# A decoder layer on one core: accumulating DMAs that read HBM, another choice of low parts made by DMA, and a single block split earlier

## The chip, the core and the metric

The kernel runs on one core of a Trainium2 chip. A core has TensorE (PE: matmuls, with weight loads, PEld, beside them), VectorE (DVE), ScalarE (ACT), GpSimd (POOL) and SyncE (SP), which only issues DMAs here; 16 DMA engines move data between HBM and the core's memory for all queues. Each engine works through its own instructions in the order in which they stand. The metric is the device time of one execution in microseconds, the median of several runs; lower is better.

## The reference

One layer of a decoder: heads of attention beside a convolution branch, an output projection, and a gated feed-forward part. All is float32; a batch of 1, 256 tokens, width 1024, feed-forward width 2816.

```python
def reference(x, norm1_g, w_in, glu_b, ..., w_out, norm2_g, w_gate, w_up, w_down):
    h = rms_norm(x, norm1_g[l])
    proj = h @ w_in[l]
    ...
    x = x + jnp.concatenate([attn, conv], axis=-1) @ w_out[l]
    h = rms_norm(x, norm2_g[l])
    x = x + (jax.nn.silu(h @ w_gate[l]) * (h @ w_up[l])) @ w_down[l]
    return x
```

The change touches the last line: `w_gate`, `w_up` and `w_down`.

## The kernel before

**Two parts of each number.** TensorE multiplies in a rounded float32 form. To keep float32 accuracy the kernel splits each operand into a high part (rounded) and a low part (what is left), and multiplies high by high, low by high and high by low. So each weight passes through three steps: a load from HBM into a raw place, the high part `wh` by ScalarE (L257), and the low part `wl`. The low part is made in one of two ways in `low_part`: VectorE subtracts (L219, raw less `wh`), or, for the pieces listed in `BY_DMA`, ScalarE writes the negated high part into `wl` (L216), and a DMA issued by GpSimd adds the raw weights to it (L217, `accum_op=add`). Before, that DMA reads the raw place.

**Pieces, blocks and places.** All weights lie in one HBM tensor `w` as 47 blocks of 128 x 2048, and a piece is 128 x 1024, so two pieces to a block. Blocks go into four raw places in turn (`RAW`), so block n + 4 overwrites block n: its load, on SyncE's queue (L196), waits until all that read block n are done, and the later loads stand behind it. High and low parts go into eight places (`WGT`); a new piece takes the one whose piece is oldest. Pieces 0 to 27 are for the projections, 28 to 71 for gate and up (a piece is one tile of 128 columns of one of them, in 22 steps `f`), and from `DOWN` = 72 on for the down projection.

**The down projection** goes in 11 pairs of 256 rows. The pairs marked F in `PAIRS` are done in seven products instead of eight (a scheme of Strassen's kind): three pieces and a *single block* of 512 columns. The first piece is the raw second half of the block; the other two are sums of blocks, the tile `t` that VectorE builds with three additions (`add_up`, L234 to L236). The single block is split by `single` (L200 on ScalarE for the high part, L201 on VectorE for the low), into `b11` for the even F pairs and into parts of the tile `other` for the rest. `single` also asks for the load of the block four further on. The P pairs have two plain pieces. Pair p uses block 36 + p:

| pair | kind | pieces | pair | kind | pieces |
|---|---|---|---|---|---|
| 0 | F | 72 to 74 | 6 | F | 88 to 90 |
| 1 | F | 75 to 77 | 7 | F | 91 to 93 |
| 2 | P | 78, 79 | 8 | F | 94 to 96 |
| 3 | F | 80 to 82 | 9 | F | 97 to 99 |
| 4 | F | 83 to 85 | 10 | P | 100, 101 |
| 5 | P | 86, 87 | | | |

**What sets the order.** The order is that in which the Python code writes the instructions; `keep_order` nails it down per engine. `feed(upto, more)` is called at every step of the products: it first makes the high parts (and, for `BY_DMA`, also the negated copy and the DMA) of pieces that lie `more` ahead, in the order of the list `turns`, and then the subtractions for all pieces up to `upto`, in the order of the pieces. `turns` is the order of the pieces, but for those in `BEHIND`: `91: 87` means that 91 has its turn right after 87, so that its DMA has longer. The tile `other` lies in the same memory as the activations of gate and up, so the first write to it waits until the last of their matmuls is done. In a product of an F pair (`seventh`) two matmuls use the high weights and a third the low ones; pair 9, the last F pair, starts with the product of its single block, the others have it as their third.

Of the kernel before, what the change touches and what calls it, by code (L numbers as in the profile page):

```python
# [8 lines left out]
F32 = mybir.dt.float32  # L9
F32R = mybir.dt.float32r  # L10
# [3 lines left out]
ALU = mybir.AluOpType  # L14
# [11 lines left out]
NF = FF // P  # L26
# [4 lines left out]
BW = 2048  # L31
PIECE = 1024
# [29 lines left out]
FAST = [p for p in range(NF // 2) if PAIRS[p] == "F"]  # L62
PLAIN = [p for p in range(NF // 2) if PAIRS[p] == "P"]
DOWN = 72
BEHIND = {83: 79, 86: 82, 88: 85, 91: 87, 94: 90, 97: 93}
BY_DMA = [*range(45, DOWN, 3), *BEHIND]
FAR = 46
SUMS = {66: 0, 69: 1}
FORMS_LATE = 11
# [66 lines left out]
def build(nc, tc, t):  # L136
    with ExitStack() as ctx:
        _build(nc, tc, t, ctx)
    keep_order(nc, tc)


def _build(nc, tc, t, ctx):
# [10 lines left out]
    def mm_bank(name, cols=512):  # L153
        return psum.tile([P, cols], F32, name=name, tag="mm", bufs=4)

    def t_bank(name, tag="t"):
        return psum.tile([P, 512], F32, name=name, tag=tag, bufs=2)
# [15 lines left out]
    def spawn(gen, wait=0):  # L173
        tasks.append([now[0] + wait, gen])

    def step():
        for task in list(tasks):
            while task in tasks and task[0] <= now[0]:
                try:
                    task[0] = now[0] + next(task[1])  # L180
                except StopIteration:
                    tasks.remove(task)
        now[0] += 1
# [4 lines left out]
    def load_block(i, between=None):  # L188
        if i >= NB:
            return  # L190
        r = raw.tile([P, BW], F32, name=f"raw{i}", tag="raw")
        n = BW // (2 if between else 1)
        for j in range(BW // n):
            if j:
                between()
            nc.sync.dma_start(r[:, j * n:(j + 1) * n], t["w"][i - 2][:, j * n:(j + 1) * n])  # L196
        blocks[i] = r

    def split(dst, src, eng):
        nc.scalar.activation(dst[0], src, AF.Copy)  # L200
        eng.tensor_tensor(dst[1], src, dst[0].bitcast(F32), op=ALU.subtract)  # L201

    def new_piece():
        j = turns[len(pieces)]
        z = places.index(min(places))
        places[z] = j
        pieces[j] = [wgt.tile([P, PIECE], F32R, name=f"w{s}{j}", tag=f"w{s}{z}") for s in "hl"]
        i, a = divmod(j * PIECE, BW)
        if j >= DOWN:
            return pieces[j], down_piece(*down[j - DOWN]), j  # L210
        return pieces[j], blocks[i][:, a:a + PIECE] if i > 1 else None, j

    def low_part(dst, src, by_dma=False):

        if by_dma:
            nc.scalar.activation(dst[1], dst[0].bitcast(F32), AF.Copy, scale=-1.0)  # L216
            nc.gpsimd.dma_start(dst[1].bitcast(F32), src, accum_op=ALU.add)  # L217
        else:
            nc.vector.tensor_tensor(dst[1], src, dst[0].bitcast(F32), op=ALU.subtract)  # L219

# [3 lines left out]
    down = [(p, a) for p in range(NF // 2) for a in range(3 if p in FAST else 2)]  # L224
    index = {d: DOWN + a for a, d in enumerate(down)}
    turns = sorted(range(DOWN + len(down)), key=lambda j: BEHIND[j] + 0.5 if j in BEHIND else j)
    wsums, b11 = {}, {}

    def add_up(q):

        if q not in wsums:
            w = blocks[DOWN // 2 + FAST[q]]
            u = wsums[q] = keep.tile([P, 4 * W], F32, name=f"t{q}", tag="big_" + "hl"[q % 2])
            nc.vector.tensor_tensor(u[:, 0:2 * W], w[:, 0:2 * W], w[:, W:3 * W], op=ALU.add)  # L234
            nc.vector.tensor_tensor(u[:, 2 * W:3 * W], u[:, 0:W], w[:, 2 * W:3 * W], op=ALU.add)
            nc.vector.tensor_tensor(u[:, 3 * W:], u[:, 2 * W:3 * W], w[:, 3 * W:], op=ALU.add)  # L236

    def down_piece(p, a):
# [5 lines left out]
        add_up(FAST.index(p))  # L244
        return wsums[FAST.index(p)][:, (2 * a - 2) * W:2 * a * W]

    def single(q):

        i = DOWN // 2 + FAST[q]
        split(b11[q if q in b11 else q % 2], blocks[i][:, 0:W], nc.vector)  # L250
        load_block(i + RAW)

    def feed(upto, more=1):
        last = DOWN + len(down) - 1
        while len(pieces) <= min(upto + more, last):
            dst, src, j = new_piece()
            nc.scalar.activation(dst[0], src, AF.Copy)  # L257
            if j in BY_DMA:
                low_part(dst, src, True)
            waiting.append((dst, src, j))  # L260
            waiting.sort(key=lambda w: w[2])
        while waiting and waiting[0][2] <= upto:
            dst, src, j = waiting.pop(0)
            if j not in BY_DMA:
                low_part(dst, src)
            if j < DOWN and j % 2:
                load_block(j // 2 + RAW)
            elif j >= DOWN and down[j - DOWN][0] in PLAIN and down[j - DOWN][1]:
                load_block(DOWN // 2 + down[j - DOWN][0] + RAW)

    def wtile(col, width):
        j, c = divmod(col, PIECE)
        return [p[:, c:c + width] for p in pieces[j]]

    def mm2(jobs, first, last):

        seen, left = set(), {}
        for z, *_ in jobs:  # L280
            left[z] = left.get(z, 0) + 1
        for z, out, w, both in jobs:
            left[z] -= 1
            nc.tensor.matmul(out.rearrange("p (a q) -> p a q", a=2), w[0], both, start=z in first and z not in seen,  # L284
                             stop=False)
            nc.tensor.matmul(out[:, 0:T], w[1], both[:, 0, :], start=False, stop=z in last and left[z] == 0)  # L286
            seen.add(z)
# [85 lines left out]
    for kt in range(KT):  # L373
        if kt % 2 == 0:
            dst, _, _ = new_piece()
# [312 lines left out]
    for chunk in range(5):  # L688
        banks = [mm_bank(f"p{chunk}{i}") for i in range(NT)]
        for kt in range(KT):  # L690
# [5 lines left out]
            w = wtile(unit * W, W)  # L696
# [175 lines left out]
    for f in range(NF):  # L872
        pg = t_bank("fg2", "s") if f == 2 else mm_bank(f"fg{f}")
        pu = mm_bank(f"fu{f}") if f < 3 else t_bank(f"fu{f}", "s")
        groups = [[(z, k) for k in range(KT)] for z in range(2)]
        if f == 0:
            groups = [[(z, k) for k in range(4)] for z in range(2)] + [[(z, k) for k in range(4, KT) for z in range(2)]]
        a = 0
        for g, group in enumerate(groups):
            jobs = []  # L880
            for z, k in group:
                if a % 4 == 0:
                    if f == a == 0:
                        step()
                    now_at = (off + a * P) // PIECE
                    if now_at in SUMS and a % 8 == 4:
                        add_up(SUMS[now_at])
                    feed(now_at + LEAD - (f == 0 and a < 12) + (now_at >= FAR))
                    if f or a:
                        step()  # L890
                if f and a == KT:
                    spawn(glu_task(f, pg, pu))
                    ffn["up"][f] = now[0] + 2
                jobs.append((z, (pg, pu)[z], wtile(off + (z * KT + k) * P, P), xg[:, :, k, :]))
                a += 1
            mm2(jobs, [z for z, k in group if k == 0], [z for z, k in group if k == KT - 1])
        if f == NF - 2:
            single(0)
        if f == 0:
            spawn(glu_task(0, pg, pu), GLU0_WAIT)  # L900
            ffn["up"][0] = now[0] + GLU0_WAIT
        off += 2 * KT * P
# [48 lines left out]
    for pair in range(NF // 2 - 1):  # L951
        for q in range(1, len(FAST)):
            if FAST[q] == pair + 1:
                single(q)
        if pair in PLAIN:
            for a in range(2):
                feed(index[pair, a] + LEAD + 1)
                plain(pair, a, dict(enumerate((M2, N3, N4, C22))))
        else:
            q = FAST.index(pair)  # L960
            groups = ((M2, N3, M1), (N5, M7), (M6, N4)) if q < len(FAST) - 1 else ((M1, N5), (M7, M6), (M2, N3, N4))
            for part, ms in enumerate(groups):
                feed(index[pair, part] + LEAD + 1)
                step()
                for m in ms:
                    seventh(q, m)
# [26 lines left out]
    for z, m in enumerate((M2, N3, N4, "left", "right")):  # L993
        step()
        i, n = divmod(min(z, 3), 2)
# [60 lines left out]
```

## Time and profile before

| what | value |
|---|---|
| three runs | 288.81, 290.47 and 290.96 us; median 290.47 |
| the profiled execution, its own time | 290.93 us |
| its span, first to last instruction | 289.1 us |
| TensorE's granted clock, mean of the span | 0.994 of full |
| VectorE busy | 238.1 us (82%), 422 instructions |
| ScalarE busy | 201.1 us (70%), 329 instructions |
| GpSimd busy | 41.6 us (14%), 69 instructions |
| read from HBM | 55.40 MB |
| high parts, L257 (raw weights) | 82 at 1050 ns |
| low parts by VectorE, L219 (raw weights) | 67 at 1218 ns |
| low parts by DMA, L217 | 15, landing 4.7 to 11.4 us after the issue, median 6.7 |

Everything outside the span (290.93 - 289.1 = 1.8 us) belongs to the start and the end of the program. "Busy" counts the time in which an engine executes; an engine can be idle because nothing is left to do or because it waits, and an answer of the trace puts in brackets how long it was idle before a row and what ended the wait.

The rows of the trace are read like this: start in us from the span's start, duration in us, engine, line, operation, what is written `<-` what is read, shape and type, and how many such instructions follow each other. Rows that overlap by some 0.1 us on one engine are pipelined. "DMA to landing" is the time from the issue of a DMA to the last of its completion signals.

Gate and up run from about 104 to 226.6 us, the down projection from there to 285.7.

### The profile page before, as it was taken

What the parts mean: (1) busy time and instruction counts of PE and PEld (TensorE: products, weight loads), DVE (VectorE), ACT (ScalarE), POOL (GpSimd) and SP (SyncE); (2) the same over time, 40 slices, a digit from 0 to 9 for tenths busy, and PEclk for the clock granted to TensorE, in tenths of its full rate; (3) what the DMA queues carried; (4) which work ended last, traced back from release to release, by engine and by line L of the source; (5) the groups of instructions that cost most, each with busy time, mean ns of one, the idle gap of its engine ahead of it and who ended that gap; (6) DMA issues with size and microseconds to landing.
All of it is one profiled execution on the core that took longest, in us unless ns stands there. A gap on an engine that the chain in (4) does not pass through costs nothing.

```text
span 289.1 us, 4132 instructions
## 1 busy us (share of the span) xinstructions
PE 282.4 (98%) x1466; PEld 236.1 (82%) x1466; DVE 238.1 (82%) x422; ACT 201.1 (70%) x329; POOL 41.6 (14%) x69
## 2 busy tenths in 40 slices
PE   8999999999999999999999999999999999996995
PEld 6888877788788888888888888888888888785884
DVE  3979995896985869999779865878799979899965
ACT  4857678996739675665879777787645667987640
POOL 0005464423000000000111111110000011121042
PEclk9999999999999999999999999999999999998999
DMA  6999958736013952565749999998960683999203
GB/s 241 407 424 344 406 203 293 276 145 261 32 20 141 383 185 67 227 226 212 215 162 274 315 262 335 232 337 198 236 275 0 204 281 100 300 245 281 45 0 145
DMA packets 12630, 64.57 MB, mean 223 GB/s; under 512 B 1665, under 2 KB 2273, under 8 KB 6978
## 3 DMA queue, kind: packets, MB, share of 16 engines
q1 hardware_dynamic: 10018, 55.14, 52.0%
q0 software_dynamic: 2448, 9.17, 15.7%
q8 instruction: 11, 0.18, 0.2%
q14 instruction: 9, 0.07, 0.1%
q10 hardware_dynamic: 144, 0.00, 0.0%
HBM read 55.40 MB, written 1.05 MB: 195 GB/s over the span
## 4 chain that ended last, share of the span: by engine, by line
PE 76%; issue 9%; DMA 7%; DVE 6%; ACT 0%; POOL 0%; POOLq 0%
PE p L701 20%; PE fg L284 12%; PE fu L284 12%; PE po L747 8%; PE sum L924 7%; PE fg L286 6%; PE fu L286 6%; DMA wl<-raw 4%; DVE wl L219 2%; DMA raw<-w 2%; PE S L535 1%; DMA first<-first 1%; PE pT L565 1%; DVE t L234 1%; PE O L721 1%
## 5 line engine op out<-in xcount | busy, mean ns | idle before, releaser
L257 ACT ACTIVATE wh<-raw 128x1024 fp32r<-128x1024 f32 x82 | 84.7, 1050 | 2.1 <-DMA raw<-w 2.1
L219 DVE TENSOR_TENSOR wl<-raw,wh 128x1024 fp32r<-128x1024 f32 x67 | 80.8, 1218 | 5.7 <-ACT wh L257 5.7
L284 PE MATMUL fu<-g,wh 128*128 128x512 f32 x176 | 62.5, 395 | 0.0
L284 PE MATMUL fg<-g,wh 128*128 128x512 f32 x176 | 62.4, 394 | 0.0
L286 PE MATMUL fg<-g,wl 128*128 128x256 f32 x176 | 48.8, 277 | 0.0
L286 PE MATMUL fu<-g,wl 128*128 128x256 f32 x176 | 48.8, 277 | 0.0
L217 POOL DMA_DIRECT2D wl<-raw x15 | 12.9, 863 | 183.9 <-ACT sf L834 82.7
L284 PEld LDWEIGHTS fg<-g,wh 128*128 128x128 f32 x176 | 33.0, 187 | 7.8 <-DVE g L768 0.2
L284 PEld LDWEIGHTS fu<-g,wh 128*128 128x128 f32 x176 | 33.0, 188 | 7.6
L286 PEld LDWEIGHTS fg<-g,wl 128*128 128x128 f32 x176 | 33.0, 188 | 0.0
L286 PEld LDWEIGHTS fu<-g,wl 128*128 128x128 f32 x176 | 33.0, 188 | 0.0
L924 PE MATMUL sum<-wh,forms 128*128 128x512 f32 x84 | 26.6, 398 | 0.0
L701 PE MATMUL p<-wh,xh 128*128 128x512 f32 x80 | 26.2, 410 | 0.1
L257 ACT ACTIVATE wh<-t 128x1024 fp32r<-128x1024 f32 x16 | 16.9, 1058 | 12.4 <-DVE t L234 11.1
L701 PE MATMUL p<-wh,xl 128*128 128x512 f32 x80 | 24.8, 391 | 0.0
L701 PE MATMUL p<-wl,xh 128*128 128x512 f32 x80 | 24.7, 390 | 0.0
L219 DVE TENSOR_TENSOR wl<-t,wh 128x1024 fp32r<-128x1024 f32 x16 | 19.5, 1217 | 0.1
L924 PE MATMUL sum<-wl,forms 128*128 128x512 f32 x42 | 17.0, 404 | 2.2 <-DMA wl<-raw 2.2
L924 PEld LDWEIGHTS sum<-wh,forms 128*128 128x128 f32 x84 | 16.3, 194 | 3.5
L701 PEld LDWEIGHTS p<-wh,xh 128*128 128x128 f32 x80 | 14.5, 191 | 4.4 <-issue 1.0
L701 PEld LDWEIGHTS p<-wh,xl 128*128 128x128 f32 x80 | 15.2, 190 | 3.4
L701 PEld LDWEIGHTS p<-wl,xh 128*128 128x128 f32 x80 | 15.0, 188 | 3.3
(203 smaller groups left out, 479.7 us busy)
## 6 DMA issues: line engine op xcount, KB each, us to landing
raw<-w SPq DMA_DIRECT2D x44, 1024.0 KB, 5.8
wl<-raw POOLq DMA_DIRECT2D x15, 512.0 KB, 6.7
first<-first SPq DMA_DIRECT2D x8, 384.0 KB, 6.5
raw<-w SPq DMA_DIRECT2D x2, 512.0 KB, 7.0
xtok<-xtok SPq DMA_DIRECT2D x2, 512.0 KB, 8.8
x<-xtok SPq DMA_DIRECT2D x2, 512.0 KB, 5.9
c_rows<-rows SPq DMA_DIRECT2D x1, 768.0 KB, 10.5
out<-x SPq DMA_DIRECT2D x3, 256.0 KB, 2.0
```

Source lines behind the costliest of these rows:

```text
L217: nc.gpsimd.dma_start(dst[1].bitcast(F32), src, accum_op=ALU.add)
L219: nc.vector.tensor_tensor(dst[1], src, dst[0].bitcast(F32), op=ALU.subtract)
L234: nc.vector.tensor_tensor(u[:, 0:2 * W], w[:, 0:2 * W], w[:, W:3 * W], op=ALU.add)
L257: nc.scalar.activation(dst[0], src, AF.Copy)
L284: nc.tensor.matmul(out.rearrange("p (a q) -> p a q", a=2), w[0], both, start=z in first and z not in seen, stop=False)
L286: nc.tensor.matmul(out[:, 0:T], w[1], both[:, 0, :], start=False, stop=z in last and left[z] == 0)
L535: nc.tensor.matmul(banks[a][:, out], G["qT"][rows, j, q], G["kT"][rows, j, k], start=True, stop=True)
L565: nc.tensor.transpose(b[:, a * P:(a + 1) * P], p[:, a * P:(a + 1) * P], ident)
L701: nc.tensor.matmul(banks[i], (xh, xh, xl)[a][:, kt, sls[i]], w[a % 2], start=kt == 0 and a == 0, stop=kt == KT - 1 and a == 1)
L721: nc.tensor.matmul(o, vs[:, 0, hs], G["pT"][h][:, 0:T], start=True, stop=False)
L747: nc.tensor.matmul(po[i, n], G["mix"][l][:, k, i * P:(i + 1) * P], w[r], start=k == a == 0, stop=k == KT - 1 and a == 2)
L924: nc.tensor.matmul(banks[m], lhs, rhs, start=first, stop=last)
```

## The change

```diff
 DOWN = 72
-BEHIND = {83: 79, 86: 82, 88: 85, 91: 87, 94: 90, 97: 93}
-BY_DMA = [*range(45, DOWN, 3), *BEHIND]
+BEHIND = {75: 72, 78: 74, 83: 79, 86: 82, 88: 85, 94: 90, 97: 93}
+BY_DMA = [*range(45, DOWN, 3), 71, *BEHIND]
...
             nc.scalar.activation(dst[1], dst[0].bitcast(F32), AF.Copy, scale=-1.0)
-            nc.gpsimd.dma_start(dst[1].bitcast(F32), src, accum_op=ALU.add)
+            nc.gpsimd.dma_start(dst[1], src.bitcast(F32R), accum_op=ALU.add)
...
+    def home(j):
+
+        i, a = divmod(j * PIECE, BW)
+        if j >= DOWN:
+            p, a = down[j - DOWN]
+            i, a = DOWN // 2 + p, (a if p in PLAIN else 1) * PIECE
+        return t["w"][i - 2][:, a:a + PIECE]
+
...
             if j in BY_DMA:
-                low_part(dst, src, True)
+                low_part(dst, home(j), True)
...
-        if f == NF - 2:
+        if f == NF - 3:
             single(0)
```

There are four edits in it.

1. The DMA that adds the raw weights takes them from HBM: `home` gives the piece's place in the tensor `w`. Both sides of it are now given as float32r, the rounded form, where both were float32. For all 17 pieces the raw place is then read by ScalarE only (and by VectorE where it makes sums or the single block of the same block).
2. Pieces 71, 75 and 78 get their low part by DMA. 75 has its turn right after 72 and 78 right after 74.
3. Piece 91 gets its low part by subtraction, in its own turn.
4. The single block of pair 0 is split after step `f` = 19 of gate and up instead of after 20.

On GpSimd, the last DMAs before the final additions read in their first form (`wl` and `wh` with the piece's number, `raw` with the block's):

```order
L217 DMA wl69_2249<-raw34_2042 128x1024
L217 DMA wl83_2555<-raw40_2456 128x1024
L217 DMA wl86_2618<-raw41_2517 128x1024
L217 DMA wl88_2675<-raw42_2560 128x1024
L217 DMA wl91_2698<-raw43_2615 128x1024
L217 DMA wl94_2740<-raw44_2659 128x1024
L217 DMA wl97_2792<-raw45_2689 128x1024
```

and in the second:

```order
L217 DMA wl69_2249<-w 128x1024
L217 DMA wl71_2308<-w 128x1024
L217 DMA wl75_2373<-w 128x1024
L217 DMA wl78_2464<-w 128x1024
L217 DMA wl83_2558<-w 128x1024
L217 DMA wl86_2621<-w 128x1024
L217 DMA wl88_2678<-w 128x1024
L217 DMA wl94_2727<-w 128x1024
L217 DMA wl97_2794<-w 128x1024
```

Three are new, 91's is gone, and none names a raw place.

On ScalarE, around pair 6 in the down projection (`t4` and `t5` are the sums of pairs 6 and 7, `b11h` the high part of pair 6's single block), the order before is:

```order
L257 ACTIVATE wh87_2685<-raw41_2517 128x1024
L257 ACTIVATE wh91_2697<-raw43_2615 128x1024
L216 ACTIVATE wl91_2698<-wh91_2697 128x1024
L257 ACTIVATE wh89_2711<-t4_2713 128x1024
L257 ACTIVATE wh90_2725<-t4_2713 128x1024
L200 ACTIVATE b11h_1077<-raw42_2560 128x512
L257 ACTIVATE wh94_2739<-raw44_2659 128x1024
L216 ACTIVATE wl94_2740<-wh94_2739 128x1024
L257 ACTIVATE wh92_2756<-t5_2758 128x1024
```

and now (L265 is the former L257):

```order
L265 ACTIVATE wh87_2688<-raw41_2521 128x1024
L265 ACTIVATE wh89_2700<-t4_2702 128x1024
L265 ACTIVATE wh90_2716<-t4_2702 128x1024
L265 ACTIVATE wh94_2726<-raw44_2662 128x1024
L216 ACTIVATE wl94_2727<-wh94_2726 128x1024
L200 ACTIVATE b11h_1077<-raw42_2563 128x512
L265 ACTIVATE wh91_2742<-raw43_2618 128x1024
L265 ACTIVATE wh92_2758<-t5_2760 128x1024
```

91's negated copy is gone, 91's high part stands behind 90's, and 94's high part and its negated copy have moved ahead of the single block of pair 6.

On VectorE the same place reads before:

```order
L219 TENSOR_TENSOR wl90_2726<-t4_2713,wh90_2725 128x1024
L201 TENSOR_TENSOR b11l_1078<-raw42_2560,b11h_1077 128x512
L234 TENSOR_TENSOR t5_2758<-raw43_2615 128x1024
L235 TENSOR_TENSOR t5_2758<-t5_2758,raw43_2615 128x512
L236 TENSOR_TENSOR t5_2758<-t5_2758,raw43_2615 128x512
L219 TENSOR_TENSOR wl92_2757<-t5_2758,wh92_2756 128x1024
```

and now:

```order
L219 TENSOR_TENSOR wl90_2717<-t4_2702,wh90_2716 128x1024
L201 TENSOR_TENSOR b11l_1078<-raw42_2563,b11h_1077 128x512
L219 TENSOR_TENSOR wl91_2743<-raw43_2618,wh91_2742 128x1024
L234 TENSOR_TENSOR t5_2760<-raw43_2618 128x1024
L235 TENSOR_TENSOR t5_2760<-t5_2760,raw43_2618 128x512
L236 TENSOR_TENSOR t5_2760<-t5_2760,raw43_2618 128x512
L219 TENSOR_TENSOR wl92_2759<-t5_2760,wh92_2758 128x1024
```

One subtraction, 91's, stands between the single block of pair 6 and the sums of pair 7. Before the down projection VectorE's list is shorter by the subtractions of 71, 75 and 78.

## The prediction

> **What bounds the kernel now.** I read the busy shares first, then who waited for whom on TensorE, then that stretch as windows, then the timelines of TensorE, VectorE and ScalarE over the last 65 us.
>
> ```profile
> PE 282.4 (98%) x1466; PEld 236.1 (82%) x1466; DVE 238.1 (82%) x422; ACT 201.1 (70%) x329; POOL 41.6 (14%) x69
> ...
> PE sum L924 <- DMA wl<-raw: 2.2, 1, 2.2
> ...
> SPq L196 <- DMA wl<-raw: 66.5, 11, 10.3
> ```
>
> TensorE works for 282.4 us of a span of 289.1, so only its holes can be won. The largest inside the program is one wait of 2.2 us of a sum's matmul for a low part that a DMA makes. SyncE's queue waited 66.5 us for such DMAs, since they read the raw place that the next load overwrites. The windows show what the hole costs (columns: length, busy us of PE, PEld, DVE, ACT, POOL with their instructions, then granted clock, DMA share, GB/s):
>
> ```profile
> 258.40:261.81 3.41, 3.41 (x17) 2.83 (x16) 3.34 (x5) 2.99 (x4) 0.86 (x1) 1.00 1.00 252
> 261.81:265.22 3.41, 1.21 (x6) 0.70 (x5) 3.34 (x5) 2.48 (x3) 0.86 (x1) 1.00 1.04 326
> 265.22:268.63 3.41, 3.41 (x9) 2.64 (x9) 3.41 (x5) 1.59 (x3) 0.00 (x0) 0.50 1.05 217
> ```
>
> TensorE was busy 1.21 of 3.41 us, and in the next 3.41 us it was granted half the clock: 9 matmuls instead of 17. Half of 3.41 us, 1.7, is lost there. The DMA engines are full (share 1.0) and VectorE has 3.3 to 3.4 us of work in each 3.41. That last fact carries my forecast. TensorE's own rows, the first at the start of piece 71, the second the last of gate and up:
>
> ```profile
> 223.69 0.40 PE L284 MATMUL fu<-g,wh 128*128 128x512 f32 x1
> ...
> 226.35 0.27 PE L286 MATMUL fu<-g,wl 128*128 128x256 f32 x1
> ...
> 247.56 0.61 PE L924 MATMUL sum<-other,forms 128*128 128x512 f32 x2
> 248.36 0.50 PE L924 MATMUL sum<-other,forms 128*128 128x512 f32 x1 [0.19 <-DVE other L201]
> ...
> 261.66 0.61 PE L924 MATMUL sum<-wh,forms 128*128 128x512 f32 x2
> 264.48 0.50 PE L924 MATMUL sum<-wl,forms 128*128 128x512 f32 x1 [2.20 <-DMA wl<-raw]
> ...
> 275.29 0.84 PE L924 MATMUL sum<-other 128*128 128x512 f32 x3
> 275.97 0.61 PE L924 MATMUL sum<-wh,other 128*128 128x512 f32 x2
> ...
> 285.44 0.28 PE L924 MATMUL sumright<-wl,act 128*128 128x256 f32 x1
> ```
>
> A pair in seven products is 21 matmuls. Pair 7 (pieces 91 to 93) begins at 261.66 and the last F pair, pair 9, at 275.29: 13.63 us for two pairs that take 2 x 21 x 0.2267 = 9.52 (a product of three takes 275.97 - 275.29 = 0.68). So 4.1 us are lost: the hole and the slow clock. At 248.36 the third matmul of a product, due 0.45 after its first at 247.56, comes 0.35 late and holds up what follows by 0.5 in all (estimate); it waits for VectorE's low part of a single block. Without both losses TensorE would end at 285.72 - 4.6 = 281.1.
>
> **The change, part by part.**
>
> *Low parts of 71, 75 and 78 go to DMA.* Each takes one subtraction from VectorE and gives ScalarE a negating copy (1.06 us) and GpSimd an issue (0.86 us). All three lie before 231 us.
>
> ```profile
> 226.90 0.62 ACT L200 ACTIVATE other<-raw 128x512 fp32r<-128x512 f32 x1
> ...
> 229.63 0.37 ACT L291 ACTIVATE us<-fu 128x256 f32<-128x256 f32 x1
> 231.61 0.42 ACT L849 ACTIVATE act<-ac 128x256 fp32r<-128x256 f32 x1 [1.62 <-DVE ac L846]
> ...
> 229.57 1.22 DVE L219 TENSOR_TENSOR wl<-raw,wh 128x1024 fp32r<-128x1024 f32 x1
> 230.70 0.42 DVE L292 TENSOR_TENSOR ac<-fu,us 128x256 f32<-128x256 f32 x1
> ...
> 235.05 1.23 DVE L219 TENSOR_TENSOR wl<-raw,wh 128x1024 fp32r<-128x1024 f32 x1 [2.00 <-ACT wh L257]
> ```
>
> A subtraction in a row of them costs VectorE 1.13 us (229.57 to 230.70), so it is relieved of 3 x 1.13 = 3.4 us. Little of that survives. ScalarE's copy `other` overwrites the place of the activations, so it cannot start before the last gate/up matmul is over (226.35 + 0.27, about 226.65), and behind it in ScalarE's queue stand the high parts, `us` of the last tile, `act`, and the high part of piece 80, for which VectorE idles 2.00 us. The lead is lost in that idling. What passes on: `other` starts at about 226.65 rather than 226.90, since the gate tile's copy no longer stands ahead of it (0.25), and `ac` no longer waits behind 78's subtraction: it starts when `us` ends (229.63 + 0.37) rather than at 230.70 (0.7). So from 235.05 VectorE runs **0.9 us earlier**. The two extra copies of ScalarE before that lie in its idle time.
>
> *The single block of pair 0 is split two pieces of gate/up earlier.* It frees its raw place some 6 us sooner, for block 40. The high part of piece 83, its first reader, stands behind `act` (231.61) on ScalarE, so this is worth nothing on the path. What hides it is ScalarE's order; gone, it would give at most the 0.9 again.
>
> *All low-part DMAs read HBM.* The raw places of the gate/up stage come free 3 to 6 us sooner and the loads follow. TensorE has no hole in that stage, so this wins nothing there. In the last stage the places are freed by VectorE's single-block subtractions, not by these DMAs. What the DMA costs the engines:
>
> ```profile
> q1 hardware_dynamic: 10018, 55.14, 52.0%
> q0 software_dynamic: 2448, 9.17, 15.7%
> ```
>
> Queue 0 moved 9.17 MB in 15.7% of 289.1 us, 202 GB/s, queue 1, the plain loads from HBM, 55.14 MB in 52%, 367 GB/s. So the 128 x 1024 x 4 = 0.524 MB of one accumulation take 2.6 us of all engines. No row shows an accumulation that reads HBM; the lower bound is a plain load of the bytes (1.4 us), the upper bound both (4.0). I take 2.6, as the nearest kind of row has it. The earliest needed of the three, 71's, is issued some 210 us in and has until 223.69, longer than the longest landing below, 11.4 us; 75's and 78's have more. Hence zero for TensorE.
>
> *91 goes back to VectorE; 94's copies go ahead of the single block on ScalarE.* These are on the path.
>
> ```profile
> 253.07 0.86 POOL L217 DMA_DIRECT2D wl<-raw  x1 [2.14 <-ACT wl L216]
> DMA to landing us min/median/max: 11.4/11.4/11.4
> ...
> 258.59 0.86 POOL L217 DMA_DIRECT2D wl<-raw  x1 [4.66 <-ACT wl L216]
> DMA to landing us min/median/max: 9.9/9.9/9.9
> ...
> 254.67 1.06 ACT L257 ACTIVATE wh<-t 128x1024 fp32r<-128x1024 f32 x1 [0.39 <-DVE t L236]
> 255.64 0.62 ACT L200 ACTIVATE b11h<-raw 128x512 fp32r<-128x512 f32 x1
> 256.16 1.05 ACT L257 ACTIVATE wh<-raw 128x1024 fp32r<-128x1024 f32 x1
> 257.24 1.06 ACT L216 ACTIVATE wl<-wh 128x1024 fp32r<-128x1024 f32 x1
> ...
> 272.16 0.61 ACT L200 ACTIVATE other<-raw 128x512 fp32r<-128x512 f32 x1
> ```
>
> ```profile
> 247.62 0.69 DVE L201 TENSOR_TENSOR other<-raw,other 128x512 fp32r<-128x512 f32 x1
> ...
> 256.91 0.68 DVE L201 TENSOR_TENSOR b11l<-raw,b11h 128x512 fp32r<-128x512 f32 x1
> 257.51 1.22 DVE L234 TENSOR_TENSOR t<-raw 128x1024 f32<-128x1024 f32 x1
> ...
> 261.23 0.68 DVE L201 TENSOR_TENSOR other<-raw,other 128x512 fp32r<-128x512 f32 x1
> ...
> 266.69 0.68 DVE L201 TENSOR_TENSOR b11l<-raw,b11h 128x512 fp32r<-128x512 f32 x1
> ...
> 272.81 0.69 DVE L201 TENSOR_TENSOR other<-raw,other 128x512 fp32r<-128x512 f32 x1 [0.57 <-ACT other L200]
> ```
>
> 91's DMA, issued at 253.07, landed 11.4 us later, at 264.4; that wait goes. (The second DMA is 94's.) Now ScalarE does 90's high part at 254.67 - 0.9 = 253.8, 94's at 254.7, its negated copy at 255.8, and only then the single block of pair 6 (256.8 to 257.4), then 91's high part (to 258.3). VectorE could take the single block at 256.91 - 0.9 = 256.0 and waits 1.4 us for it, then subtracts 91 from 258.36 on (1.13). The sum `t` of pair 7 then starts at 259.5 instead of 257.51: from there VectorE is **2.0 us later** than before, and behind it all its rows touch.
>
> The low part of pair 7's single block comes at 263.9 (261.91 + 2.0). TensorE, rid of the hole at 248, begins pair 7 at 261.2 and wants it eight matmuls later, at 263.0: a wait of about 1.0. Pair 8's comes at 269.4, wanted at 268.7: 0.7. Pair 9 begins with its single block: TensorE is there at 272.4, ScalarE's half is ready at 274.8 (272.77 + 2.0), VectorE's at 275.5 (273.50 + 2.0): waits of 2.4 and 0.3. From the third matmul of that block (275.74 before) to the end took 9.98 us, so TensorE ends at 275.5 + 0.05 + 9.98 = 285.5, against 285.72: **0.2 us earlier**. The 4.6 us gained come back as 4.4 us of waits for VectorE.
>
> **Does the clock fall again?** The row says that a window with 2.2 us idle halved the next. A wait of 2.4 and 0.3 us close together would do the same if it falls in one window, and cost 1.7. How the windows lie to the program differs between executions; the runs of before, 288.81 to 290.96, differ by about this much. I take it as lost.
>
> The Trainium skill, TensorE: Matmul & The Clock Gate, in its section "Part 1: The HAM clock gate", says that the clock halves after an idle window of about 3.4 us, which runs free of the program. The trace agrees on the window (3.41 us at 0.50) and not on the idleness: 1.21 us of work in it did not save the clock. By the page's words the new wait would cost no clock, and the sum would be that of the first rival.
>
> **Sum.** The profiled execution took 290.93 us, 0.46 above the median of 290.47. 290.93 - 0.2 + 1.7 = **292.4 us**, where its own 1.7 stands within the 4.6 that were taken off.
>
> **Rivals.**
> 1. *The same waits, the clock kept.* 290.93 - 0.2 = 290.7. For it: the wait is split in two, and a window's edge can part it further. Against: it is longer than the one that cost the clock.
> 2. *VectorE's lead lasts, faster.* If VectorE gets into the last stage with its 3.4 us, all waits shrink below 1 us and the time is 290.93 - 4.6 = 286.3. For it: that stage waits for VectorE throughout. Against: the 2.00 us it idles at 235.05 for ScalarE, which no edit shortens by more than 0.9. It decides from a lead of about 3 us at the sums of pair 3.
> 3. *Block 44 late, slower.* 94's high part now stands ahead of the single block, and it needs block 44, issued when VectorE is done with pair 4's single block (248.31 before, 247.4 now). The landings of that load before and of the next but one:
>
> ```profile
> DMA to landing us min/median/max: 5.2/5.2/5.2
> ...
> DMA to landing us min/median/max: 10.0/10.0/10.0
> ```
>
> The first ran beside one accumulation, the second beside two. From a landing of 7.3 us on (254.7 - 247.4), each us delays ScalarE, VectorE and the end; at 10.0 it is 2.7, so 295.1. For it: accumulations from HBM at 4.0 us. Against: only one of them, 88's, then runs beside it.
> 4. *The wait moves to 94's DMA instead, so the change doesn't do what it says.* That DMA landed at 268.5 (258.59 + 9.9), and TensorE now wants it by 267.4 (pair 8's start at 266.9, two matmuls on). It is issued some 1.6 us earlier and has one rival less, and a wait of 1 us there would only eat into the wait of 2.4 behind it: 290.9 to 292.4.
>
> **Chances.** Forecast 0.45; rival 1 0.25; rival 2 0.17; rival 3 0.08; rival 4 0.05. A measurement of this kernel tells about 1% from no change: 287.6 and 293.4 are the edges. Faster takes rival 2 but for its upper end, 0.16; slower takes rival 3 and the forecast's upper end, 0.15; the same is 0.69. For 8 in 10 the range takes in the forecast, rivals 1 and 4 and the near half of 2 and 3: 287.0 to 294.0; the likeliest case by itself spans 291.4 to 293.4.
>
> **What would show it.** No wait of TensorE for a DMA near 262; instead waits for VectorE's or ScalarE's single blocks (L201, L200 of before) at pairs 7, 8 and 9, the last over 2 us, and a window at 0.50 clock right behind it. VectorE idle over 1 us ahead of pair 6's single block, its last low part some 2 us later than 276.9. More VectorE idling before 235. I am wrong if VectorE's subtractions from 235 on run 2 us earlier than before, or if TensorE waits over 1 us for block 44's or 94's transfers.

## The result and the profile after

The changed kernel takes 292.18 us (median of 14 runs, 290.53 to 292.88) against 289.83 us of the kernel before (14 runs on the same chip, 288.61 to 291.0): a ratio of 1.0071, interval 1.0046 to 1.0097. That is slower, by less than 1%. The profiled execution took 292.5 us with a span of 290.7. All lines of the code from L247 on are 8 higher than before: L924 is now L932, L257 is L265, L971 is L979.

The busy shares of the page hardly differ from those of before. VectorE, which was relieved of a net two subtractions (420 instructions after 422), is busy 1.9 us less, and the end comes later all the same.

```profile
PE 283.4 (97%) x1466; PEld 236.1 (81%) x1466; DVE 236.2 (81%) x420; ACT 202.7 (70%) x331; POOL 44.1 (15%) x71
```

TensorE's rows show what took the place of the wait for 91's DMA (start, duration, then in brackets the idle time ahead of the row and what ended it). The first row is the last matmul of gate and up, the last row TensorE's last matmul:

```profile
226.46 0.27 PE L294 MATMUL fu<-g,wl 128*128 128x256 f32 x1
...
264.10 0.50 PE L932 MATMUL sum<-other,forms 128*128 128x512 f32 x1 [0.49 <-DVE other L201]
269.56 0.50 PE L932 MATMUL sum<-b11l,forms 128*128 128x512 f32 x1 [0.40 <-DVE b11l L201]
274.95 1.32 PE L932 MATMUL sum<-other 128*128 128x512 f32 x3 [2.15 <-ACT other L200]
...
287.08 0.28 PE L932 MATMUL sumright<-wl,act 128*128 128x256 f32 x1
```

No row waits for a DMA near 262. There are three waits for single blocks, at pairs 7, 8 and 9, and the last is the long one. VectorE's rows of the same execution say why: the first is the low part of piece 80, the next three are the single block of pair 6, piece 91 and the first sum of pair 7, then the single block of pair 9 and the last two low parts.

```profile
234.27 1.23 DVE L219 TENSOR_TENSOR wl<-raw,wh 128x1024 fp32r<-128x1024 f32 x1 [2.01 <-ACT wh L265]
...
257.55 0.69 DVE L201 TENSOR_TENSOR b11l<-raw,b11h 128x512 fp32r<-128x512 f32 x1 [1.34 <-ACT b11h L200]
258.50 1.23 DVE L219 TENSOR_TENSOR wl<-raw,wh 128x1024 fp32r<-128x1024 f32 x1 [0.26 <-ACT wh L265]
259.64 1.22 DVE L234 TENSOR_TENSOR t<-raw 128x1024 f32<-128x1024 f32 x1
...
274.93 0.69 DVE L201 TENSOR_TENSOR other<-raw,other 128x512 fp32r<-128x512 f32 x1 [0.57 <-ACT other L200]
...
276.68 2.35 DVE L219 TENSOR_TENSOR wl<-raw,wh 128x1024 fp32r<-128x1024 f32 x2
```

At 234.27 VectorE is 0.78 us ahead of before (235.05). Gate and up did not end at the same time in both executions: their last matmul starts at 226.46, before at 226.35, and in the twelve profiles of this study anywhere from 225.91 to 226.84. Counted from that matmul, piece 80 comes after 7.81 us instead of 8.70, so the lead is 0.89 us. Between two executions, bare times can therefore be off by some tenths of a us, and where it matters below I count from that matmul. VectorE stands idle for 1.34 us at 257.55 and then subtracts 91, so that the sum starts at 259.64 instead of 257.51. Its last low part ends at 276.68 + 2.35 = 279.03, 2.1 us later than before (274.55 + 2.35 = 276.90), or 2.0 us counted as above. ScalarE's rows hold the cause of the idle time: 94's high part, its negated copy, and only then the half of the single block that VectorE wants.

```profile
254.86 1.05 ACT L265 ACTIVATE wh<-raw 128x1024 fp32r<-128x1024 f32 x1
255.94 1.06 ACT L216 ACTIVATE wl<-wh 128x1024 fp32r<-128x1024 f32 x1
256.90 0.61 ACT L200 ACTIVATE b11h<-raw 128x512 fp32r<-128x512 f32 x1
```

The windows of 3.41 us (length, busy us of PE, PEld, DVE, ACT and POOL, then granted clock, DMA share, GB/s) have the same picture around pair 9 as the kernel before had around 262:

```profile
272.50:275.91 3.41, 1.26 (x5) 0.53 (x4) 2.81 (x5) 3.02 (x5) 0.00 (x0) 1.00 0.00 0
275.91:279.32 3.41, 3.41 (x9) 2.67 (x9) 3.12 (x3) 2.09 (x3) 1.20 (x1) 0.50 0.00 0
279.32:282.73 3.41, 3.41 (x16) 2.83 (x16) 2.04 (x3) 1.96 (x3) 2.07 (x2) 1.00 0.00 0
```

9 matmuls at half the clock, 16 at the full one. Such a window lowers the mean granted clock of an execution by 3.41 x 0.5 / 290.7 = 0.006, and so the executions can be sorted by their clock. Of the 14 of the changed kernel, 4 have a clock of 0.997 or more, with a median of 290.6 us; the 10 others have 292.3. I call the first sort *unhalved* below and compare it with its like, since both kernels have both sorts.

### The profile page after: what moved, and what is told of

The parts are those of the page before. It is cut to its first block, busy times and chain, and to the rows that moved or that the text cites. A ratio compares the mean times of both kernels' runs of the same rounds, so it can differ in the third digit from the quotient of the medians.

```text
span 290.7 us, 4120 instructions
## 1 busy us (share of the span) xinstructions
PE 283.4 (97%) x1466; PEld 236.1 (81%) x1466; DVE 236.2 (81%) x420; ACT 202.7 (70%) x331; POOL 44.1 (15%) x71
## 3 DMA queue, kind: packets, MB, share of 16 engines
q0 software_dynamic: 2736, 10.22, 18.2%
## 4 chain that ended last, share of the span: by engine, by line
PE 90%; DVE 4%; issue 2%; ACT 1%; DMA 1%; ACTq 0%; DVEq 0%
PE p L709 19%; PE fg L292 14%; PE fu L292 14%; PE sum L932 13%; PE po L755 8%; PE fg L294 7%; PE fu L294 7%; DVE wl L219 1%; DVE t L234 1%; PE S L543 1%; DMA first<-first 1%; PE pT L573 1%; DVE t L235 1%; ACT wh L265 1%; PE O L729 1%
## 5 line engine op out<-in xcount | busy, mean ns | idle before, releaser
L265 ACT ACTIVATE wh<-raw 128x1024 fp32r<-128x1024 f32 x82 | 84.8, 1051 | 3.5 <-DMA raw<-w 3.5
L219 DVE TENSOR_TENSOR wl<-raw,wh 128x1024 fp32r<-128x1024 f32 x65 | 78.4, 1220 | 6.0 <-ACT wh L265 6.0
L217 POOL DMA_DIRECT2D wl<-w x17 | 14.7, 865 | 184.2 <-ACT sf L842 76.6
L265 ACT ACTIVATE wh<-t 128x1024 fp32r<-128x1024 f32 x16 | 16.9, 1056 | 13.4 <-DVE t L234 12.3
L932 PE MATMUL sum<-wh,forms 128*128 128x512 f32 x84 | 25.9, 390 | 0.0
L216 ACT ACTIVATE wl<-wh 128x1024 fp32r<-128x1024 f32 x17 | 18.1, 1062 | 0.5
L932 PEld LDWEIGHTS sum<-wh,forms 128*128 128x128 f32 x84 | 15.7, 188 | 3.2
```

The lines of the kernel that those rows point to most:

```text
L217: nc.gpsimd.dma_start(dst[1], src.bitcast(F32R), accum_op=ALU.add)
L932: nc.tensor.matmul(banks[m], lhs, rhs, start=first, stop=last)
```

## Experiments

Ratios and intervals are to the kernel before, run beside it on the same chip; "unhalved" medians are added with their count.

**The HBM source alone**

```diff
-                low_part(dst, src, True)
+                low_part(dst, home(j), True)
```

(the kernel before, with `home` and the float32r types of the DMA, and nothing else)

> The kernel before, with only the source of the low-part DMAs changed: they read the piece's home in HBM, not its raw place. My theory (the time came from 91's return to VectorE and from 94's copies standing ahead of pair 6's single block on ScalarE): this edit alone does next to nothing, 289.4 to 290.6 us against 289.8 of before; the last stage still has the wait of about 2 us for 91's DMA near 262, and VectorE's last low part still ends near 277. Rival A (the DMAs from HBM crowd the engines and delay the loads of blocks): this alone is slower by the whole 2.3 us, 291.5 or more, and loads land later.

288.99 us, ratio 0.9991 (0.9959 to 1.0023): no difference, and rival A falls. The rest of the expectation was half right. VectorE's rows stayed (its last low part ends at 276.71), but the wait of 2 us for 91's DMA isn't there. In TensorE's rows of this kernel, and in one of its weight loads (the third row), the low parts of 88 and 91 and the single block of pair 9 are waited for:

```profile
257.68 0.50 PE L932 MATMUL sum<-wl,forms 128*128 128x512 f32 x1 [0.35 <-DMA wl<-w]
...
272.63 1.23 PE L932 MATMUL sum<-other 128*128 128x512 f32 x3 [0.56 <-ACT other L200]
```

```profile
262.68 0.19 PEld L932 LDWEIGHTS sum<-wl,forms 128*128 128x128 f32 x1 [0.37 <-DMA wl<-w]
```

91's DMA took 9.8 us to land here, 11.4 in the profile of before; 88's took 7.8, before 5.9. What is no longer waited for at 91 is waited for at pair 9 in part, since VectorE is no earlier. Whether the shorter wait for 91 comes from the source isn't shown: there is one profile of each kernel, and that of before is of an execution that lost the clock.

**91 to VectorE alone**

```diff
-BEHIND = {83: 79, 86: 82, 88: 85, 91: 87, 94: 90, 97: 93}
+BEHIND = {83: 79, 86: 82, 88: 85, 94: 90, 97: 93}
```

> The kernel before, with only 91 taken out of the table of DMA pieces: VectorE subtracts it, and 94's high part and negated copy stand ahead of pair 6's single block on ScalarE. My theory: the whole loss and a little more, since VectorE lacks the 0.8 us of lead that the three other pieces gave: 292.5 to 293.5 us; VectorE idles about 1.3 us ahead of pair 6's single block, its last low part ends 2.5 to 3 us later than 276.9, and TensorE waits about 3 us at pair 9's single block. Rivals A (HBM source) and B (more DMAs of 71, 75, 78 crowd the stage before): about as before, 289.8, or faster, since 91's wait is gone and nothing was put in its place.

293.28 us, ratio 1.011 (1.0063 to 1.0158): the whole loss and more, from this edit by itself. VectorE's single block of pair 6 and its last low parts, and TensorE's wait at pair 9:

```profile
258.82 0.69 DVE L201 TENSOR_TENSOR b11l<-raw,b11h 128x512 fp32r<-128x512 f32 x1 [1.33 <-ACT b11h L200]
...
277.94 2.36 DVE L219 TENSOR_TENSOR wl<-raw,wh 128x1024 fp32r<-128x1024 f32 x2
```

```profile
276.22 1.23 PE L924 MATMUL sum<-other 128*128 128x512 f32 x3 [2.15 <-ACT other L200]
```

The idle time is the expected 1.33 us. The last low part ends at 280.30, 3.4 us later than before, but the last matmul of gate and up starts 0.5 us later too (226.84), which this edit doesn't touch; from there on it is 2.9 us, within the 2.5 to 3 that I had. The wait at pair 9 is 2.15 us and not 3, since the waits at pairs 7 and 8 (0.70 and 0.39 us) had already held TensorE up.

**91 by DMA again, all else as changed**

```diff
-BEHIND = {75: 72, 78: 74, 83: 79, 86: 82, 88: 85, 94: 90, 97: 93}
+BEHIND = {75: 72, 78: 74, 83: 79, 86: 82, 88: 85, 91: 87, 94: 90, 97: 93}
```

> The changed kernel with 91 put back among the DMA pieces, so that all its other edits stand alone. My theory: VectorE gets its 1.1 us of subtraction back and keeps the lead of 0.8; the single block of pair 6 still stands behind copies on ScalarE as in the kernel before. The time is that of before or a little better, 288.8 to 290.3 us, with a wait of 1.5 to 3 us for 91's DMA near 262, as before. Rivals A and B: 291.5 or more, since the HBM source and the three DMAs are still in.

287.96 us, ratio 0.9947 (0.9916 to 0.9977): faster than before, and better than I expected. So the other three edits do no harm together. 91's wait was 0.71 us where I had 1.5 to 3:

```profile
262.11 0.50 PE L932 MATMUL sum<-wl,forms 128*128 128x512 f32 x1 [0.71 <-DMA wl<-w]
```

**94's copies behind the single block**

```diff
-BEHIND = {75: 72, 78: 74, 83: 79, 86: 82, 88: 85, 94: 90, 97: 93}
+BEHIND = {75: 72, 78: 74, 83: 79, 86: 82, 88: 85, 94: 91, 97: 93}
```

> The changed kernel with 94's turn moved from behind 90 to behind 91: its high part and negated copy now stand behind pair 6's single block on ScalarE, 91's high part ahead of it. My theory: VectorE's idle time of 1.34 us ahead of that single block shrinks to 0.3 or less, all its rows behind come 1.0 to 1.3 us sooner, TensorE's waits at pair 9 add up to about 1.5 us instead of 2.7, and the clock isn't lost in most executions: 289.3 to 291.0 us. Rival C (what costs is 91's subtraction itself, 1.2 us, not the order on ScalarE): 291.5 to 292.5, VectorE's last low part where it was (279.0). A new risk: 94's DMA is issued about 1.7 us later, and its landing could be waited for near 267.

289.62 us, ratio 0.9995 (0.9965 to 1.0026). One turn on ScalarE undoes most of the loss, with 91 still subtracted by VectorE; rival C falls as it stood. The two rows of VectorE are the single block of pair 6 and the last low parts:

```profile
256.54 0.69 DVE L201 TENSOR_TENSOR b11l<-raw,b11h 128x512 fp32r<-128x512 f32 x1 [0.24 <-ACT b11h L200]
...
275.33 2.35 DVE L219 TENSOR_TENSOR wl<-raw,wh 128x1024 fp32r<-128x1024 f32 x2
```

Its idle time fell from 1.34 to 0.24 us, and the end of its low parts from 279.03 to 277.68. Unhalved, 289.5 us (9 of 12), against 290.6 of the changed kernel: the order costs about 1.1 us. Against 288.9 of the kernel before (20 of 29) 0.6 us remain, which the ratio hides since the kernel before lost the clock more often in this set; 91's subtraction itself isn't free. The wait at pair 9 was again 2.15 us, not the 1.5 that I expected, because TensorE no longer waits at pairs 7 and 8 and comes to pair 9 sooner. 94's DMA wasn't waited for.

**Work in the wait: does the clock fall for idleness?**

```diff
+            for _ in range(16 if q == len(FAST) - 1 else 0):
+                nc.tensor.matmul(banks[M1][:, 0:T], nought, ones, start=False, stop=False)
             groups = ((M2, N3, M1), (N5, M7), (M6, N4)) if q < len(FAST) - 1 else ((M1, N5), (M7, M6), (M2, N3, N4))
```

(the changed kernel; `nought` is a tile of zeros that GpSimd sets at the start)

> The changed kernel with 16 matmuls that add nothing (all-zero bf16 weights, 256 columns, into the open bank of the first sum) put on TensorE just ahead of pair 9, where it waits 2.15 us for the single block. They take some 2 us and fit into the wait; nothing that is computed changes. My theory (the slow clock behind this wait is caused by the idleness, and costs 1.7 us where it falls): the granted clock is 0.998 to 1.0 in every execution and the median comes down from 292.2 to 290.4 to 290.9 us, where the undisturbed executions of the changed kernel already lie (290.5 to 290.8). Rival (the clock falls for another reason, or the time between the two groups comes from elsewhere): the same two groups of executions as without them, median 292.

290.93 us, and the changed kernel on the same chip:

> The changed kernel again, as the standard for the other runs of this set: 291.5 to 292.8 us.

291.23 us (290.81 to 293.37), a median that falls between its two sorts: 5 of its 12 executions are unhalved. (The clock doesn't tell the time in every case: two of the 7 others took 290.82 and 291.17 us, no longer than the unhalved ones.) With the added matmuls 11 of 12 are unhalved. The rows show them in the wait:

```profile
272.28 1.95 PE L972 MATMUL sum<-const-bfloat16-1.0,nought 128*128 128x256 bf16 x16
274.58 1.23 PE L934 MATMUL sum<-other 128*128 128x512 f32 x3 [0.35 <-ACT other L200]
```

The wait ends no sooner than in the changed kernel's second profile: from the last matmul of gate and up it is 274.58 - 226.09 = 48.49 us, there 274.90 - 226.42 = 48.48. And yet one of 12 has a lower clock (292.1 us), where 7 of 12 have it without the matmuls. So the lower clock goes with TensorE's idling in this wait. The other kernels bear it out: of those whose profile has no wait of TensorE above 0.71 us in the down projection (HBM source alone, 91 by DMA again, and the two of the last experiment below), 2 of 48 executions lost the clock. The gain in time is small, 0.3 us in the median, as the changed kernel's median was below the forecast 291.5. Another of the 12 took 292.06 us at full clock; nothing here shows why.

**Pair 0's single block put back**

```diff
-        if f == NF - 3:
+        if f == NF - 2:
             single(0)
```

> The changed kernel with only the single block of pair 0 put back to where it was split before. My theory (that edit moves nothing on the path): the same as the changed kernel within 0.3 us, 291.5 to 292.8, the waits at pairs 7, 8 and 9 unchanged. Rival (it takes part in the lead or the loss): 0.5 us or more away from it, VectorE's rows from 235 on shifted by as much.

291.7 us, ratio 1.0073 (1.0043 to 1.0103), beside 1.0066 (1.0036 to 1.0097) of the changed kernel in the same set. Over all executions that is no difference that can be told. Unhalved it is 291.3 us (7) against 290.9 (5), with ranges that overlap, and the trace does show an effect. The rows are the last matmul of gate and up, the high part of piece 83 on ScalarE, and VectorE's low part of 80:

```profile
225.91 0.27 PE L294 MATMUL fu<-g,wl 128*128 128x256 f32 x1
...
230.96 1.06 ACT L265 ACTIVATE wh<-raw 128x1024 fp32r<-128x1024 f32 x1 [0.26 <-PE sum L932]
...
234.09 1.23 DVE L219 TENSOR_TENSOR wl<-raw,wh 128x1024 fp32r<-128x1024 f32 x1 [2.38 <-ACT wh L265]
```

From that matmul to the low part it is 8.18 us, in the changed kernel 7.81 (7.80 to 7.83 in all seven profiles that have the three DMAs and the early split). So 0.37 us of the lead go, and pair 9 begins that much later as well: 274.77 - 225.91 = 48.86 us against 48.48. ScalarE waits at piece 83: its high part starts 5.05 us after that matmul, in the changed kernel 4.69 (231.15 - 226.46) and without a wait. The bracket names TensorE, but TensorE runs through pair 0 without a hole in both; the likelier cause is the load of block 40, from which 83 is read. Its last completion signal in the trace comes at 230.87, 9.0 us after its issue at 221.85, beside 78's accumulation, issued at 221.20. With the early split it is issued before that accumulation and lands by 223.6. This is the rival's mechanism, at 0.4 us instead of its 0.5.

**71, 75 and 78 by DMA alone**

```diff
-BEHIND = {83: 79, 86: 82, 88: 85, 91: 87, 94: 90, 97: 93}
-BY_DMA = [*range(45, DOWN, 3), *BEHIND]
+BEHIND = {75: 72, 78: 74, 83: 79, 86: 82, 88: 85, 91: 87, 94: 90, 97: 93}
+BY_DMA = [*range(45, DOWN, 3), 71, *BEHIND]
```

> The kernel before with only the low parts of 71, 75 and 78 given to DMAs, which still read the raw places; 91 stays a DMA, pair 0's single block where it was. My theory: of the 3.4 us of relief, VectorE keeps 0.8 to 1.0 from 235 on, as in the changed kernel; the time is 0.5 to 1.2 us below that of before, 288.0 to 288.7. Rival 1 (the lead needs the HBM source, since DMAs that read raw places hold up the loads): as before or slower, 289.2 or more. Rival 2 (the whole 3.4 us pass on): 286 to 287.

288.04 us, ratio 0.998 (0.9945 to 1.0015). Over all executions that can't be told from before. Unhalved, it is 287.94 us (7, none above 288.06) against 288.98 (21, none below 288.30): 1.0 us faster. The relief passes on in part, but less of it than I expected: VectorE's low part of 80 starts at 234.31, which is 0.74 us sooner than in the profile of before, but only 0.51 sooner when counted from the last matmul of gate and up (8.19 us after 226.12, before 8.70). It comes after more idling, as with pair 0's single block put back; here too block 40's load lands late, at 231.1:

```profile
234.31 1.23 DVE L219 TENSOR_TENSOR wl<-raw,wh 128x1024 fp32r<-128x1024 f32 x1 [2.39 <-ACT wh L257]
```

**Pair 9's single block split earlier**

Two kernels, one with 91 by DMA, one with 94's copies behind the single block; both call `single` for pair 9 inside pair 7, so that ScalarE and VectorE split that block ahead of the high parts and sums of pair 9:

```diff
-        for q in range(1, len(FAST)):
+        for q in range(1, len(FAST) - 1):
...
                 feed(index[pair, part] + LEAD + 1)
+                single(len(FAST) - 1) if q == len(FAST) - 3 and part == 0 else None
```

> The changed kernel with 91 by DMA again (as in e3_91_by_dma_again, 287.96 us) and pair 9's single block split earlier: on ScalarE ahead of the high parts of 98 and 99, on VectorE ahead of pair 9's sums, not behind them. My theory: VectorE loses the 0.57 us in which it waits for ScalarE's half of that block, the last waits of TensorE at pair 9 (0.5 us of weight loads) go, and the time is 287.0 to 287.7. What is left is 91's DMA at pair 7. Rival (pair 9 no longer matters once 91 is a DMA): 287.9 as without it. A risk: 96's low part comes 0.6 us later; it had 3.1 us to spare.

287.56 us, ratio 0.9927 (0.9892 to 0.9962), all 12 executions unhalved (286.87 to 289.84): the best version of this study. The list of who waited for whom holds only these for the sums, 0.3 us each, of TensorE's weight loads:

```profile
PEld sum L932 <- DMA wl<-w: 0.3, 1, 0.3
PEld sum L932 <- DVE wl L219: 0.3, 1, 0.3
```

> The changed kernel with 94's copies behind pair 6's single block (as in e4_94_behind_single, 289.62 us) and pair 9's single block split earlier, as in the other run of this set. 91 is subtracted by VectorE. My theory: the 2.15 us in which TensorE waits there stand for one block that is split behind work it does not need; split ahead, TensorE waits less than 0.8 us at pair 9, and the time is 287.4 to 288.4. Rival (VectorE is so late by then that 98 or 99 is waited for in place of the single block): 289.0 to 289.6, with waits for low parts of 98 or 99 in the rows.

288.92 us, ratio 0.9971 (0.9943 to 1.0): 0.7 us better than without the earlier split (in another set; the kernel before is at 288.9 unhalved in both), all 12 unhalved, but short of what I expected. The rival's mechanism holds: 98's low part is waited for instead.

```profile
273.54 0.50 PE L932 MATMUL sum<-wl,other 128*128 128x512 f32 x1 [0.70 <-DVE wl L219]
```

That low part ends at 273.49. With VectorE late, the wait moves to the next thing it makes; only taking 91 off it (287.56) removes the wait.

## Why the prediction was right, point by point

**The time.** 292.18 us were measured against 292.4. TensorE's last matmul ends at 287.08 + 0.28 = 287.36; the working had 285.5 and 1.7 for the clock, 287.2. The path came out as worked. That the median lies within 0.2 us of the forecast is in part luck: it depends on how many executions lose the clock, and with 7 of 12 instead of 10 of 14 the second set had 291.23, between the forecast and rival 1.

**71, 75, 78: a lead of 0.9 us out of 3.4.** The size came out, 0.89 us counted from the last matmul of gate and up, but not from this edit alone: by itself it gives 0.51, and the other 0.38 need the early split of pair 0's single block. The reason why most of the relief is lost held: ScalarE's copy `other` waits for the last matmul of gate and up, and VectorE then for ScalarE. A row of the changed kernel's ScalarE has the first of them:

```profile
226.77 0.63 ACT L200 ACTIVATE other<-raw 128x512 fp32r<-128x512 f32 x1 [1.08 <-PE fu L294]
```

I had 226.65. What the prediction didn't say is that this edit by itself is faster by 1.0 us in time, unhalved. The lead of 0.5 would account for half of that; the rest isn't explained.

**Pair 0's single block: not nothing.** This step of the working was wrong, by about 0.4 us. It held that block 40 is there in time anyway, since piece 83 stands behind `act` on ScalarE. That is so in the kernel before, where the load lands at 228.2 and ScalarE comes to 83 at 231.94, but not in the two kernels that have the three DMAs and the late split: there ScalarE waits at piece 83, and with one edit between them (pair 0's single block put back) VectorE and pair 9 come 0.37 us later. As both edits were made together, the forecast of 0.9 wasn't hurt by it.

**HBM as the source: no gain, 2.6 us of the engines for one accumulation.** The edit alone gives a ratio of 0.9991. The price, in the changed kernel:

```profile
q0 software_dynamic: 2736, 10.22, 18.2%
```

10.22 MB in 18.2% of 290.7 us is 193 GB/s, 2.7 us for 0.524 MB (8.9 of the 10.22 MB are accumulations). Zero for TensorE was a little too little: it waits for 88's low part, with a weight load for 0.5 us in the first profile of the changed kernel and with a matmul for 0.7 in the second. 88's DMA landed 5.6 to 6.0 us after its issue in the three profiles that read the raw place, and 5.9 to 8.5 us after it in the nine that read HBM. These waits lie ahead of the long one and shorten it.

**91 and 94's order: VectorE 2.0 us later from pair 7 on.** Of the two parts, the idle time was 1.34 us (1.4 in the working), and the sum of pair 7 started at 259.64 (259.5). The last low part ends 2.0 us later, counted from the last matmul of gate and up. The waits of TensorE were 0.49, 0.40 and 2.15 us plus about 0.5 inside the block, against 1.0, 0.7, 2.4 and 0.3 of the working: smaller, since 88's wait had come first and TensorE came later to each, with the same end. The experiments with single edits give this step its proof: alone it is slower by 1.1%; giving 91 back to a DMA makes the kernel 1.0 us faster than before, and putting 94's copies back behind the single block leaves it 0.6 us slower (both unhalved).

**The clock halved again: 1.7 us.** It was in the profiled execution and in 10 of 14, and 292.3 - 290.6 = 1.7 us separate the two sorts. The Trainium skill, TensorE: Matmul & The Clock Gate, "Part 1: The HAM clock gate", has the clock halve after an idle window of about 3.4 us that runs free of the program. The windows here agree with the length, and they fit the free running, as only some executions of one program lose the clock at the same wait. They don't agree with "idle": 1.26 us of work in 3.41 didn't keep the clock, and 16 matmuls more did.

**Where the working was loose.** It set "0.2 us earlier" against an execution of before that had itself lost 1.7 us to the clock. Like with like, the change costs 290.6 - 288.9 = 1.7 us unhalved (288.9 is the median of 20 unhalved executions of before in another set; in the set that has both kernels it is 290.9 - 289.0 = 1.9). The parts roughly add up: 91 and its order alone cost 3.1 us (292.0 of only two unhalved executions, less 288.9), the three DMAs alone give back 1.0, pair 0's single block some 0.4, the HBM source nothing. Beyond that, the changed kernel loses the clock more often: 17 of its 26 executions, 31 of the 87 of before.

**The rivals.** The first (same waits, clock kept, 290.7) is what the unhalved executions are: 290.6 in one set, 290.9 in the other. The second (the lead of 3.4 us lasts) falls with the 0.89. The third (block 44 late) doesn't show: 94's high part starts at 254.86 right behind the copy ahead of it, with no wait. The fourth neither: 94's DMA, issued at 257.29, landed at 263.09, and pair 8, which reads it, begins at 267.19.

**What stays open.** 91's DMA took 11.4 us to land in the profile of before and 9.4 to 10.4 in the four other profiles that have it. From HBM it took 10.3 us (91 by DMA again) and from the raw place 10.4 (71, 75 and 78 alone), so the source isn't shown to be the reason. Nor is it shown how long that wait is in executions of the kernel before that keep the clock: its one profile has 2.20 us, the other kernel whose 91 reads the raw place by DMA 1.15.

## What to carry to other kernels

Work taken off an engine that is busy 82% of the time is worth only what isn't lost at its next wait for another engine: follow the queue of the engine that feeds it before counting a gain. An edit that looks worth nothing in the old kernel can be needed by another edit made beside it, as the early split was by the three DMAs. Where two engines split one block between them, look at what stands ahead of each half: here one turn of two copies cost 1.1 us, and splitting the last block before work that it didn't need won 0.4 to 0.7. And compare executions by their granted clock, since a wait of 2 us may or may not cost as much again behind it, and compare rows from an event that the change doesn't touch: gate and up ended up to 0.9 us apart here.

## What was not expected of the hardware

Behind a wait of 2.15 us the clock is halved in one execution and not in the next of the same program (10 of 14, then 7 of 12), and 16 matmuls that add zero, 1.95 us in all, keep it in 11 of 12. The queue of the accumulating DMAs moves 188 to 199 GB/s over the 16 engines in the nine profiles in which they read HBM, little less than the 201 to 203 in the three in which they read the core's own memory.
